# An SSD stage whose VectorE, ScalarE and GpSimd work is ordered by hand, with the decayed state formed one step ahead and one ring of eight PSUM banks

## The chip, the core and the metric

The kernel runs on one NeuronCore of a Trainium2 chip. The metric is the device time of one execution in microseconds. Before the change three runs gave 1432.12, 1432.25 and 1435.49 us, median 1432.25.

## The reference

One layer of a decoder trunk on an input of 1024 rows and 1024 columns, in float32. After a norm with modulation, one wide product makes all branches; a gated spatial mixer and a Mamba-2 state-space part (SSD) follow, and both are projected, gated, summed, projected again and normed. The SSD part works in chunks of 128 rows, for 8 groups of 4 heads (head width 64, state width 128):

```python
xd = (x * dt[..., None]).reshape(b, nc, q, g, r, p)
a_cs = jnp.cumsum(adt, axis=-1)
decay = segsum_exp(adt)
cb = jnp.einsum('bclgn,bcsgn->bcgls', cc, bc)
y_diag = jnp.einsum('bcgls,bcgrls,bcsgrp->bclgrp', cb, decay, xd)
chunk_states = jnp.einsum('bcsgn,bcgrs,bcsgrp->bcgrpn', bc, decay_to_end, xd)
chunk_decay = jnp.exp(a_cs[..., -1])
def step(state, inp):
    cs, cd = inp
    return state * cd[..., None, None] + cs, state
...
y_off = jnp.einsum('bclgn,bcgrpn,bcgrl->bclgrp', cc, prev_states, jnp.exp(a_cs))
```

The output is y_diag + y_off + x * d_skip, multiplied by silu(z) and normed by group. The state of a group runs through its 8 chunks: each new state is the old one times its decay plus the chunk's own sum.

## The kernel before, in words

The program has five stages. Up to about 930 us it norms and modulates the input and forms the wide product; each product is cut into 7 smaller ones (a Strassen scheme, function pair), and every operand is split into a high and a low fp32r half, so that a product is three matmuls. From about 930 to 1150 us runs the **SSD stage**, up to about 1180 us its end, up to about 1335 us the product with w_proj_b (units p1, p2, p5 and so on), and then the output.

The SSD stage is a loop over 32 steps (the list order, L1098). A step is one group and one pair of chunks, i = 0 and 1; two groups alternate, so that a group comes back every second step. A step has these parts:

- fetch (L951, on SP's queue) loads dcy (the cumulated decays, spread over 128 partitions) and sl (B, C, x and z of the step).
- decay (L956): ScalarE forms ea, the exponentials for y_off (L961); GpSimd masks the triangle (affine_select, L964); ScalarE exponentiates dcy in eight pieces (L969).
- prep (L971): TensorE forms the product of B and C and the transposes into the banks pc and px; VectorE multiplies dcy by pc (L989) and x by its two weights, into xd and xe (L985); ScalarE copies bn from pc (L991).
- front (L994): TensorE multiplies yi (the diagonal part, 16 small matmuls) and sp (the two chunk sums). For each of the two new states GpSimd multiplies the old state by its decay (L1017) and VectorE adds sp (L1019). The first state of a group is a copy (L1015).
- back (L1023): TensorE multiplies yn from the states; evacuate (L1036): VectorE forms y1 = x * d_skip + yi (L1045) and ym = yn * ea (L1049); GpSimd adds them (y, L1050) and multiplies by z (yz, L1051).
- post (L1053, every second step of a group): ScalarE's queue stores yz to DRAM (L88); by later(n, ...), a list of due times counted in slots, the squares follow (ScalarE L1069, GpSimd's sum L1070), then a product with ones into pq and the mean ssq (post2, VectorE L1077), and after a group's last pair the power -1/2 on GpSimd (L1081) and a transpose pr of the row (post3).

Between these parts TensorE draws filler (draw): the product of the gated branch with w_proj_a (proj_a; block dd has 48 matmuls into two banks pma, and two loads tha, which VectorE scales by pma at L1270 and ScalarE's queue stores). The weights of the next block are split into wah (ScalarE, L1171) and wal (VectorE, L1172). Behind the loop the last filler (draw(left[0] - 5), and five pieces at the end) runs while the first units of w_proj_b are made ready: load yn and p1r, norm yn (L1376), the halves p1bh, p1bl (L1415, L1416) and p1a (L1420, L1421), then twelve matmuls of a unit into four banks x0 to x3 (L1437).

What sets the order: pin keeps an instruction in program order on its engine. All matmuls and transposes (mm L76, tp L79) and all loads on SP (L85) are pinned. VectorE, ScalarE and GpSimd work of the SSD stage is not pinned: a scheduler orders it at build time by its own estimate of the times, with high_priority for the parts of a step. Whatever the order is, each engine executes its queue strictly in it.

PSUM: the pool ps1 has six banks with the tag bk and two with the tag px. In the SSD stage every fourth call of bank takes a px bank. The states of all groups share four places by turns (st_r). The rings y1_r, ym_r, ea_r, tha_r, war_r, wah_r, wal_r hand out buffers by turns (turn).

Of the kernel before, what the change touches and what calls it, by code (L numbers as in the profile page):

```python
# [8 lines left out]
F32 = mybir.dt.float32  # L9
# [26 lines left out]
def hybrid_kernel(  # L36
# [7 lines left out]
    V, A, G, PE = nc.vector, nc.scalar, nc.gpsimd, nc.tensor  # L44
# [42 lines left out]
    def store(dst, src):  # L87
        nc.scalar.dma_start(dst, src)  # L88
# [478 lines left out]
    pending, pairs_done = [], []  # L567
# [366 lines left out]
    class Group:  # L934


        def __init__(self, g):
            self.g, self.pre, self.st, self.yz, self.y = g, {}, None, {}, {}
# [17 lines left out]
        def decay(self, s):  # L956

            g = self.g
            sl, dcy, ea = self.pre[s]
            for hh in range(2):  # L960
                A.activation(ea[hh * HD : (hh + 1) * HD],  # L961
                             dcy.rearrange("p (j e) i l -> p e j (i l)", e=2)[hh * HD : (hh + 1) * HD, hh], AF.Exp)
            d8 = dcy.rearrange("p h i l -> p (h i) l")
            G.affine_select(out=d8, in_=d8, compare_op=ALU.is_ge, fill=-1e30, base=0,  # L964
                            pattern=[[0, 2 * HPG], [1, P]], channel_multiplier=-1)
            sub = fac(nacs, g, s)
# [4 lines left out]
        def prep(self, s):  # L971
            g, nm = self.g, f"{self.g}_{s}"
# [8 lines left out]
            x4 = px.rearrange("p (i h w) -> p i h w", i=2, h=HPG)  # L981
            xs = []
            for v, f in (("xd", dthq), ("xe", dde)):
                t = p2x.tile([P, 512], F32, name=f"{v}{nm}", tag=v, bufs=3)
                V.tensor_tensor(t.rearrange("p (i h w) -> p i h w", i=2, h=HPG), x4,  # L985
                                fac(f, g, s).unsqueeze(3).to_broadcast([P, 2, HPG, HD]), op=ALU.mult)
                xs.append(t)
            d3 = dcy.rearrange("p h i l -> p h (i l)")
            V.tensor_tensor(d3, d3, pc[:, 0:256].unsqueeze(1).to_broadcast([P, HPG, 256]), op=ALU.mult)  # L989
            bn = p2x.tile([P, 256], F32, name=f"bn{nm}", tag="bn", bufs=3)  # L990
            A.copy(bn, pc[:, 256:512])  # L991
            self.pre[s] = (sl, dcy, bn, xs[0], xs[1], ea)

        def front(self, s):  # L994

            g, nm = self.g, f"{self.g}_{s}"
            sl, dcy, bn, xd, xe, ea = self.pre[s]
            v3 = lambda t: t.rearrange("p (h w) -> p h w", h=HPG)
# [7 lines left out]
            self.y[s] = yi  # L1006
            self.sts = [self.st]
            for i in range(2 if s < NCH // 2 - 1 else 1):
                mm(sp[:, i * 256 : (i + 1) * 256], bn[:, i * P : (i + 1) * P], xe[:, i * 256 : (i + 1) * 256])
            for i in range(2 if s < NCH // 2 - 1 else 1):  # L1010
                pool, tag, b = st_r[nst[0] % 4 if nst[0] % 4 < 3 else 2]
                nst[0] += 1
                s2 = pool.tile([P, 512 if pool is hp else 256], F32, name=f"st{nm}_{i}", tag=tag, bufs=b)[:, 0:256]
                if self.st is None:
                    V.tensor_copy(s2, sp[:, 0:256])  # L1015
                else:
                    G.tensor_mul(v3(s2), v3(self.st),  # L1017
                                 fac(cd, g, s)[:, i].unsqueeze(2).to_broadcast([P, HPG, HD]))
                    V.tensor_add(s2, s2, sp[:, i * 256 : (i + 1) * 256])  # L1019
                self.st = s2  # L1020
                self.sts.append(s2)

        def back(self, s):  # L1023

            sl = self.pre[s][0]
            yn = bank(f"yn{self.g}_{s}")
# [5 lines left out]
            self.evacuate(s, self.y.pop(s), yn)  # L1032
            if s % 2:
                self.post(s // 2)

        def evacuate(self, s, yi, yn):  # L1036

            g, nm = self.g, f"{self.g}_{s}"
            sl, ea = self.pre[s][0], self.pre[s][5]
# [3 lines left out]
            y1 = turn(y1_r, f"y1{nm}", F32).rearrange("p (j t) -> p j t", j=2)  # L1043
            for j in range(2):
                V.scalar_tensor_tensor(y1[:, j], sl[:, 2 + j], dskt[:, 2 * g + j : 2 * g + j + 1],  # L1045
                                       yi[:, j * 256 : (j + 1) * 256], op0=ALU.mult, op1=ALU.add)
# [3 lines left out]
            G.tensor_add(y1[:, :, t0:], y1[:, :, t0:], m[:, :, t0:])  # L1050
            G.tensor_mul(yz, y1, sl[:, 4:6])  # L1051

        def post(self, q):  # L1053

            g = self.g
            for j in range(2):
                store(yb_d[2 * g + j][:, q * 512 : (q + 1) * 512], self.yz[q][:, j])
            yz = self.yz[q]
            if g < NG - 2 or q == 0:
                later(5, self.squares, yz, [yz[:, j] for j in range(2)])  # L1060
                later(17, self.post2, q, yz[:, 0])
            else:
                sq = [turn(r, f"sq{g}", F32) for r in (y1_r, ym_r)]
# [8 lines left out]
        def post2(self, q, sq):  # L1072
            g = self.g
            pq = bank(f"pq{g}_{q}")
            for i in range(4):
                mm(pq[:, i : i + 1], sq[:, i * P : (i + 1) * P], ones[:, 0:1])
            V.tensor_scalar(ssq[:, g * NCH + q * 4 : g * NCH + q * 4 + 4], pq[:, 0:4], 1.0 / 256, EPS,  # L1077
# [7 lines left out]
        def post3(self):  # L1085
# [6 lines left out]
            store(rs_d[g].rearrange("o (c p) -> (o c) p", p=P), row)  # L1092
# [74 lines left out]
    def wa_block(dd):  # L1167
        was[dd] = []
        for i, wr in enumerate(war.pop(dd)):
            wh, wl = turn(wah_r[0], f"wah{dd}_{i}"), turn(wal_r[0], f"wal{dd}_{i}")  # L1170
            A.copy(wh, wr)  # L1171
            V.tensor_sub(wl, wr, f32(wh))  # L1172
            was[dd].append((wh, wl))
# [73 lines left out]
    def proj_a():  # L1247

        for dd in range(KT):
# [8 lines left out]
            for k in range(KT):  # L1258
# [7 lines left out]
                if k == 1 and dd + 1 < KT:  # L1266
                    wa_block(dd + 1)
# [3 lines left out]
            for h in range(2):  # L1271
                keep(nc.scalar.dma_start(mt_d[dd][:, h * 512 : (h + 1) * 512], ths[h]))
# [4 lines left out]
    st_r = [(hp, room.pop(0), 1), (p2x, "st", 1), (p2q, "st", 2)]  # L1277
# [5 lines left out]
    pairs_done.append("")  # L1283
# [22 lines left out]

    draw(6)
# [15 lines left out]


    room.extend(ea_r[0] + [st_r[0][1]])
# [168 lines left out]
    ps1.__exit__(None, None, None)  # L1494
# [18 lines left out]
    for u, (nm, k) in enumerate(units):  # L1513
# [12 lines left out]
        if nm == "p1" and k in (4, 5):  # L1526
            groups[NG - 6 + k].post3()
# [152 lines left out]
```

## Time and profile before

| what | us |
|---|---|
| median of three runs | 1432.25 |
| span of the profiled execution | 1432.7 |
| TensorE busy in it | 1396.2 |
| VectorE, ScalarE, GpSimd busy | 1024.9, 785.1, 205.7 |
| first yi of the SSD stage | 931.90 |
| last yi | 1149.73 |
| first matmul of unit p1 (x) | 1176.17 |
| TensorE idle from 930 to 1150 | 13.5 of 220 |
| TensorE idle from 1150 to 1180 | 4.65 of 30 |

The profiled execution's span is its time from the first to the last instruction; it lies within the range of the three runs. In rows of the timeline the first number is the start and the second the duration, counted from the span's start; in brackets stands the idle time of the engine just before the row and what ended it. In rows of groups the last two parts are busy time with the mean of one, and the idle time before them by releaser. PE is TensorE, DVE is VectorE, ACT is ScalarE, POOL is GpSimd, SP is the queue that issues loads; PEld are weight loads.

### The profile page before, as it was taken

How to read it: one execution, taken by the hardware profiler on the slowest of the kernel's cores; microseconds unless marked ns; L12 is line 12 of the kernel's file. 1: busy time of each engine (PE TensorE's matmuls, PEld its weight loads, DVE VectorE, ACT ScalarE, POOL GpSimd, SP SyncE). 2: the span in 40 equal slices, each digit the busy share in tenths (PEclk: the TensorE clock that was granted, in tenths of full speed). 3: DMA queues.
4: the chain of work that ended last, by engine and by line, in shares of the span. 5: the costliest groups of instructions: out<-in, count | busy, mean ns of one | idle time of the engine just before them, and what ended most of it. 6: DMA issues, size and time to landing. Idle time of an engine off the chain costs nothing.

```text
span 1432.7 us, 20518 instructions
## 1 busy us (share of the span) xinstructions
PE 1396.2 (97%) x7087; PEld 1152.6 (80%) x7087; DVE 1024.9 (72%) x1821; ACT 785.1 (55%) x1444; POOL 205.7 (14%) x190
## 2 busy tenths in 40 slices
PE   8999999999999999999999999999989989999997
PEld 6688888888888888888887888877878877787886
DVE  5686776777667888788887784587677767948443
ACT  6664576566656565555665555776667524325101
POOL 0000000000000000000000100057878830000000
PEclk9999999999999999999999999999999999999999
DMA  8552343333332777687677764788778668977332
GB/s 266 162 162 89 118 118 103 107 100 118 103 114 86 205 223 225 190 246 215 195 231 216 220 180 142 268 297 307 254 262 295 215 211 286 352 254 284 124 118 74
DMA packets 260524, 277.08 MB, mean 193 GB/s; under 512 B 13596, under 2 KB 210628, under 8 KB 260420
## 3 DMA queue, kind: packets, MB, share of 16 engines
q1 hardware_dynamic: 179396, 195.37, 43.8%
q10 hardware_dynamic: 81024, 80.40, 16.6%
q8 instruction: 56, 0.92, 0.3%
q14 instruction: 48, 0.39, 0.1%
HBM read 191.40 MB, written 84.31 MB: 192 GB/s over the span
## 4 chain that ended last, share of the span: by engine, by line
PE 78%; DMA 8%; DVE 5%; issue 3%; ACT 3%; POOL 2%; SPq 1%; ACTq 0%; POOLq 0%; DVEq 0%
PE xuz L563 6%; PE po L76 6%; PE xcb L563 6%; PE xx L563 5%; PE xz L563 5%; PE x L1437 5%; PE xg L563 5%; PE pma L76 3%; PE yp L1437 3%; PE yuz L563 3%; PE xv L563 3%; PE ycb L563 3%; PE yx L563 3%; PE yz L563 2%; PE yg L563 2%
## 5 line engine op out<-in xcount | busy, mean ns | idle before, releaser
L770 POOL TENSOR_TENSOR wog<-wog,gb 128x1024 f32<-128x1024 f32 x8 | 21.8, 2722 | 724.8 <-PE xz L563 529.1
L969 ACT ACTIVATE dcy<-dcy,nacs 128x128 f32<-128x128 f32 x256 | 78.5, 389 | 14.4 <-POOL dcy L964 14.2
L964 POOL TENSOR_SCALAR_AFFINE_SELECT dcy<-dcy 128x1024 f32<-128x1024 f32 x32 | 35.1, 1097 | 107.8 <-ACT ea L961 104.1
L961 ACT ACTIVATE ea<-dcy 64x512 f32<-64x512 f32 x64 | 40.1, 627 | 12.6 <-DMA dcy<-acs_d 12.2
L882 ACT ACTIVATE ac<-ac 128x1024 f32<-128x1024 f32 x32 | 34.0, 1061 | 20.0 <-DVE ac L880 19.8
L1643 ACT ACTIVATE xr<-r 128x1024 f32<-128x1024 f32 x7 | 7.4, 1061 | 67.2 <-issue 39.7
L76 PE MATMUL pma<-yh,wah 128*128 128x512 f32 x128 | 43.9, 424 | 0.0
L76 PE MATMUL pma<-yh,wal 128*128 128x512 f32 x128 | 43.2, 419 | 0.0
L1049 DVE TENSOR_TENSOR ym<-yn,ea 128x512 f32<-128x512 f32 (+1 forms) x32 | 19.9, 623 | 31.3 <-PE yn L76 31.2
L1051 POOL TENSOR_TENSOR yz<-y,sl 128x512 f32<-128x512 f32 x32 | 41.9, 1309 | 1.1
L989 DVE TENSOR_TENSOR dcy<-dcy,pc 128x1024 f32<-128x1024 f32 x32 | 39.0, 1217 | 4.3 <-PE pc L79 3.0
L76 PE MATMUL pma<-yl,wah 128*128 128x512 f32 x128 | 40.5, 398 | 0.0
L76 PEld LDWEIGHTS yn<-sl,st 128*128 128x128 f32 x224 | 30.3, 190 | 10.9 <-POOL yz L1051 2.9
L1050 POOL TENSOR_TENSOR y<-y,ym 128x512 f32<-128x512 f32 (+1 forms) x32 | 36.5, 1142 | 16.3 <-DVE ym L1049 16.3
L1633 POOL TENSOR_TENSOR r<-r,fnw 128x256 f32<-128x256 f32 (+1 forms) x3 | 2.7, 916 | 250.7 <-ACT xr L1632 250.7
L76 PE MATMUL yn<-sl,st 128*128 128x128 f32 x224 | 31.7, 276 | 7.1 <-DVE st L1019 7.1
L880 DVE SCALAR_TENSOR_TENSOR ac<-c2x,cwt,ac 128x1023 f32<-128x1023 f32 (+2 forms) x24 | 31.8, 1325 | 9.0 <-ACT ac L878 7.1
L1642 DVE TENSOR_TENSOR r<-po,xr 128x1024 f32<-128x1024 f32 x7 | 8.6, 1225 | 41.1 <-PE po L76 41.1
L76 PE MATMUL sp<-xe,bn 128*128 128x256 f32 x112 | 33.0, 411 | 4.5 <-DVE ym L1049 1.4
L76 PE MATMUL yi<-dcy,xd 128*64 128x128 f32 x512 | 35.9, 284 | 0.0
L880 DVE SCALAR_TENSOR_TENSOR ac<-c2cb,cwt,ac 128x1023 f32<-128x1023 f32 (+2 forms) x24 | 30.6, 1275 | 7.1 <-ACT ac L878 7.0
L1017 POOL TENSOR_TENSOR st<-st,cd 128x256 f32<-128x256 f32 x48 | 32.3, 673 | 10.3 <-PE yn L76 7.2
(2827 smaller groups left out, 4395.4 us busy)
## 6 DMA issues: line engine op xcount, KB each, us to landing
sl<-s_d SPq DMA_DIRECT2D x32, 768.0 KB
s_d<-ac ACTq DMA_DIRECT2D x32, 512.0 KB
dcy<-acs_d SPq DMA_DIRECT2D x32, 512.0 KB
aw<-in_ada_w_dram SPq DMA_DIRECT2D x16, 512.0 KB
wbr<-in_w_proj_b_dram SPq DMA_DIRECT2D x64, 128.0 KB
wb_d<-wbb ACTq DMA_DIRECT2D x32, 256.0 KB
wb_d<-wbc ACTq DMA_DIRECT2D x32, 256.0 KB
yb_d<-yz ACTq DMA_DIRECT2D x32, 256.0 KB
```

The costliest lines, as they stand in the source:

```text
L76: pin(PE.matmul(acc, l, r, start=first, stop=last))
L563: pin(PE.matmul(ps, lw[:, k * P : (k + 1) * P], r[k], start=first and n + k == 0, stop=n == 2 and k == 3, skip_group_check=not first))
L880: V.scalar_tensor_tensor(ac[:, s:], cc[:, : S - s], conv_wt[:, 3 - s, i : i + 1], ac[:, s:], op0=ALU.mult, op1=ALU.add)
L882: A.activation(ac, ac, AF.Silu)
L961: A.activation(ea[hh * HD : (hh + 1) * HD], dcy.rearrange("p (j e) i l -> p e j (i l)", e=2)[hh * HD : (hh + 1) * HD, hh], AF.Exp)
L964: G.affine_select(out=d8, in_=d8, compare_op=ALU.is_ge, fill=-1e30, base=0, pattern=[[0, 2 * HPG], [1, P]], channel_multiplier=-1)
L969: A.activation(dcy[:, h, i, :], dcy[:, h, i, :], AF.Exp, bias=sub[:, i, h : h + 1])
L989: V.tensor_tensor(d3, d3, pc[:, 0:256].unsqueeze(1).to_broadcast([P, HPG, 256]), op=ALU.mult)
L1017: G.tensor_mul(v3(s2), v3(self.st), fac(cd, g, s)[:, i].unsqueeze(2).to_broadcast([P, HPG, HD]))
L1050: G.tensor_add(y1[:, :, t0:], y1[:, :, t0:], m[:, :, t0:])
L1051: G.tensor_mul(yz, y1, sl[:, 4:6])
L1437: pin(PE.matmul(ps[j], a[:, v, js], r, start=first and n + k == 0, stop=n == 2 and k == KT - 1, skip_group_check=not first))
```

## The change

- A wrapper Engine passes every instruction that VectorE, ScalarE and GpSimd issue inside the SSD loop through pin, as long as hand[0] is true: their order is then that of the program text (in the changed kernel's profile such an instruction has the line of the wrapper).
- decay is split into decay_rows (ea and the mask) and decay_exps, prep into prep_products (with dcy and xd), prep_b (bn) and prep_xe. The loop issues them at set places: decay_rows of step n+3 first, then front of n, xe of n+1, back of n, prep_products of n+2, decay_exps of n+3, prep_b of n+2.
- y1 is formed in front, straight behind yi, no longer in evacuate.
- The decayed state is formed one step ahead: front adds sp to a state that GpSimd has decayed before (self.nxt), and GpSimd at once decays it for chunk 1; back adds chunk 1's sum behind ym, and GpSimd decays the result for the group's next step, ahead of yz. There are five places for states instead of four.
- At the start of the stage ps1 is closed and a pool ps2 with one ring of eight banks is opened; it is laid on the same banks.
- Stores of yz, mt_d and rs_d are issued through later, squares after 9 slots instead of 5, the mean ssq one slot behind its product, and wal two filler pieces behind wah.

The core of the diff:

```diff
-    V, A, G, PE = nc.vector, nc.scalar, nc.gpsimd, nc.tensor
+    hand = [False]
+    class Engine:
+        def __getattr__(self, name):
+            f = getattr(self.e, name)
+            if not hand[0]:
+                return f
+            return lambda *a, **k: tc.keep_in_program_order(f(*a, **k))
+    V, A, G, PE = Engine(nc.vector), Engine(nc.scalar), Engine(nc.gpsimd), nc.tensor
...
-        if pairs_done:
-            pairs_done.append(name)
-            if len(pairs_done) % 4 == 2:
-                return psum.tile([P, 512], F32, name=name, tag="px", bufs=2)
-        return psum.tile([P, 512], F32, name=name, tag="bk", bufs=6)
+        return psum.tile([P, 512], F32, name=name, tag="bk", bufs=n_banks[0])
...
+    def decayed(self, dst, s, i):
+        v3 = lambda t: t.rearrange("p (h w) -> p h w", h=HPG)
+        G.tensor_mul(v3(dst), v3(self.st), fac(cd, self.g, s)[:, i].unsqueeze(2).to_broadcast([P, HPG, HD]))
...
+            if self.st is None:
+                self.st = self.state(f"st{nm}_0")
+                V.tensor_copy(self.st, sp[:, 0:256])
+            else:
+                self.st = self.nxt
+                V.tensor_add(self.st, self.st, sp[:, 0:256])
+            self.sts.append(self.st)
+            self.nxt = None
+            if not last:
+                self.nxt = self.state(f"st{nm}_1"), sp
+                self.decayed(self.nxt[0], s, 1)
...
+            if self.nxt is not None:
+                self.st, sp = self.nxt
+                V.tensor_add(self.st, self.st, sp[:, 256:512])
+                self.nxt = self.state(f"st{nm}_2")
+                self.decayed(self.nxt, s + 1, 0)
             G.tensor_mul(yz, y1, sl[:, 4:6])
...
-    pairs_done.append("")
+    ps1.__exit__(None, None, None)
+    ps2 = tc.tile_pool(name="ps2", bufs=1, space=PSUM, reuse_waits="tile")
+    psum = ps2.__enter__()
+    n_banks[0] = 8
...
+    hand[0] = True
     draw(6)
     for n in range(2):
         step(n, "front")
         draw(10)
-    for n in range(len(order)):
+    for n in range(N):
+        ahead3 = 0 < n < N - 3
+        if ahead3:
+            of(n + 3, "decay_rows")
         if n > 1:
             step(n, "front")
             draw(10 if n == 2 else 4 + n % 2)
+        if 0 < n < N - 1:
+            of(n + 1, "prep_xe")
         step(n, "back")
-        if n + 2 < len(order):
-            step(n + 2, "prep")
+        if n + 2 < N:
+            step(n + 2, "prep_products")
+        if ahead3:
+            of(n + 3, "decay_exps")
+        if n + 2 < N:
+            of(n + 2, "prep_b")
         fetch(n + 6)
-        decays(n + 4)
     while tasks:
         draw(2)
         run_tasks()
+    hand[0] = False
```

More of the change, by code (lines that the diff above doesn't have):

```diff
@@ L965, in decay, with decay_exps @@
                             pattern=[[0, 2 * HPG], [1, P]], channel_multiplier=-1)
-            sub = fac(nacs, g, s)
+        def decay_exps(self, s):
+            dcy = self.pre[s][1]
+            sub = fac(nacs, self.g, s)
             for i in range(2):
@@ L1042, in evacuate @@
             yz = self.yz[s // 2][:, :, (s % 2) * 256 : (s % 2 + 1) * 256]
[L1043 to L1046, printed above, removed]
+            y1 = self.y.pop(s)
             m = turn(ym_r, f"ym{nm}", F32).rearrange("p (j t) -> p j t", j=2)
@@ L1305, in step, with of @@
             item(getattr(groups[order[n][0]], f), order[n][1])
+    N = len(order)
+    def of(n, f):
+        g, s = order[n]
+        getattr(groups[g], f)(s)
+    hand[0] = True
     draw(6)
@@ L1526, in hybrid_kernel @@
         if nm == "p1" and k in (4, 5):
-            groups[NG - 6 + k].post3()
+            groups[NG - 6 + k].post3(True)
         if k % 2 and nm in GATES:
```

132 lines of the change are left out of this document (81 added, 51 removed).

## Prediction

> **What bounds the kernel now.** I read the page first, then the table of stretches, then TensorE's waits in the SSD stage, and last the timeline around each wait.
>
> ```profile
> span 1432.7 us, 20518 instructions
> PE 1396.2 (97%) x7087; PEld 1152.6 (80%) x7087; DVE 1024.9 (72%) x1821; ACT 785.1 (55%) x1444; POOL 205.7 (14%) x190
> ```
>
> The span lies 0.45 us above the median of the three runs (1432.25). I work against the span and take 0.45 off at the end. TensorE is busy 97%, so only its idle time can be won. The stretches (busy us of PE, PEld, DVE, ACT, POOL, then the granted clock) tell where that is:
>
> ```profile
> 930.00:1150.00 220.00, 206.48 (x1548) 178.87 (x1548) 163.32 (x294) 145.70 (x378) 162.45 (x158) 0.99 0.78 268
> 1150.00:1180.00 30.00, 25.35 (x136) 21.09 (x133) 17.04 (x32) 9.30 (x17) 11.96 (x8) 0.94 0.70 229
> 1180.00:1335.00 155.00, 153.86 (x656) 122.66 (x655) 115.31 (x185) 57.63 (x98) 0.00 (x0) 1.00 0.83 287
> ```
>
> The change touches the first two rows: 13.5 us idle in 220, and 4.65 in the 30 where the stage runs out. The product stage behind it is full, so it can neither hide a delay nor give time back. TensorE's waits from 925 to 1180 (releaser: total, times, longest):
>
> ```profile
> PE yn L76 <- DVE st L1019: 7.1, 6, 2.7
> PE pq L76 <- POOL sq L1070: 4.6, 1, 4.6
> PE pc L76 <- issue: 1.9, 1, 1.9
> PE sp L76 <- DVE ym L1049: 1.4, 1, 1.4
> PE sp L76 <- DVE xe L985: 1.2, 2, 0.6
> PE sp L76 <- DVE ssq L1077: 1.0, 1, 1.0
> PE sp L76 <- DVE st L1019: 0.9, 1, 0.9
> ```
>
> All but pq sum to 13.5: half are products that wait for a new state, the rest mostly PSUM banks that VectorE has not yet read. The timeline (start, duration) gives the frame and a second cost:
>
> ```profile
> 931.90 1.09 PE L76 MATMUL yi<-dcy,xd 128*64 128x128 f32 x16
> 949.18 0.46 PE L76 MATMUL pc<-sl 128*128 128x128 f32 x2 [1.90 <-issue]
> 984.53 0.68 PE L76 MATMUL yn<-sl,st 128*128 128x128 f32 x4 [2.72 <-DVE st L1019]
> 986.61 1.98 PE L76 MATMUL yi<-dcy,xd 128*64 128x128 f32 x16
> 1041.99 0.68 PE L76 MATMUL yn<-sl,st 128*128 128x128 f32 x4 [2.34 <-DVE st L1019]
> 1149.73 1.09 PE L76 MATMUL yi<-dcy,xd 128*64 128x128 f32 x16
> ```
>
> After the 2.72 us wait the same sixteen yi products take 1.98 instead of 1.09: the granted clock fell. With the matmuls beside them I put the loss at 1.6 us, an estimate. After 2.34 us nothing was lost. First to last yi is 217.8 us for 31 steps; without 13.5 and 1.6 it is 202.7, **6.54 us a step**, the floor that TensorE's own work sets.
>
> **The change part by part.** Instructions per engine are the same in kind and number; only order, banks and waits differ.
>
> (1) *The state one step ahead.* GpSimd multiplies the old state by its decay before the sum it belongs to exists, so yn waits only for one addition. In the built program yi(n) now waits for xe(n), sp(n) for ym(n-1), each read a step earlier. What does a step cost the other engines? The groups from 950 to 1150 (29 steps; total, mean ns):
>
> ```profile
> L1051 POOL TENSOR_TENSOR yz<-y,sl 128x512 f32<-128x512 f32 x29 | 38.0, 1311 | 1.0
> L1017 POOL TENSOR_TENSOR st<-st,cd 128x256 f32<-128x256 f32 x44 | 29.9, 679 | 8.2 <-PE yn L76 6.5 <-DVE st L1015 1.1 <-DVE st L1019 0.6
> L964 POOL TENSOR_SCALAR_AFFINE_SELECT dcy<-dcy 128x1024 f32<-128x1024 f32 x27 | 29.6, 1097 | 19.3 <-ACT ea L961 19.3
> L1050 POOL TENSOR_TENSOR y<-y,ym 128x512 f32<-128x512 f32 x22 | 28.1, 1278 | 12.7 <-DVE ym L1049 12.7
> L1050 POOL TENSOR_TENSOR y<-y,ym 128x256 f32<-128x256 f32 x7 | 5.1, 734 | 0.2 <-DVE ym L1049 0.2
> L1070 POOL TENSOR_TENSOR yz<-yz 128x512 f32<-128x512 f32 x14 | 18.0, 1283 | 4.0 <-ACT yz L1069 3.4 <-DVE st L1019 0.5
> L1081 POOL TENSOR_TENSOR ssq<-ssq,nhalf 128x8 f32<-128x8 f32 x6 | 9.9, 1653 | 0.0
> L1049 DVE TENSOR_TENSOR ym<-yn,ea 128x512 f32<-128x512 f32 x23 | 15.9, 690 | 28.0 <-PE yn L76 28.0
> L1019 DVE TENSOR_TENSOR st<-st,sp 128x256 f32<-128x256 f32 x45 | 18.5, 413 | 10.3 <-POOL st L1017 9.8 <-PE sp L76 0.4
> L989 DVE TENSOR_TENSOR dcy<-dcy,pc 128x1024 f32<-128x1024 f32 x29 | 35.3, 1217 | 3.8 <-PE pc L79 2.5 <-issue 0.7 <-ACT yz L1069 0.2
> L1045 DVE SCALAR_TENSOR_TENSOR y<-sl,dskt,yi 128x256 f32<-128x256 f32 x58 | 25.0, 473 | 0.0
> L1270 DVE SCALAR_TENSOR_TENSOR tha<-tha,pma 128x512 f32<-128x512 f32 x12 | 7.8, 682 | 0.9 <-PE pma L76 0.9
> ```
>
> And from the timeline, xd and xe of step 1, one behind the other:
>
> ```profile
> 935.27 0.68 DVE L985 TENSOR_TENSOR xd<-px,dthq 128x512 f32<-128x512 f32 x1
> 935.87 0.67 DVE L985 TENSOR_TENSOR xe<-px,dde 128x512 f32<-128x512 f32 x1
> ```
>
> GpSimd's rows sum to 158.6 us over 29, or 5.47 a step. VectorE's loop from one yn to the next, in the new order, is ym 0.69, state 0.41, dcy 1.22, xd 0.68, two y1 0.95, state 0.41: 4.36, against 6.54 less yn's own 0.9, or 5.65. Both fit, so the 13.5 and the 1.6 go: **-15.1**.
>
> (2) *What the fixed order leaves.* In seven steps the two tha (1.36) stand in that loop: 4.36 + 1.36 is 5.72, over by 0.07, and by up to 0.7 with xe behind them. In three steps squares (1.28) and the power (1.65) meet on GpSimd: the affine 1.10, two decays 1.36, y 1.28, yz 1.31 and these are 7.98, 1.44 over 6.54; the state addition st1 on VectorE then waits, with dcy, xd and the next yn behind it. Bounds: 0 to 7 x 0.7 + 3 x 1.44 = 9.2. I take half of what the sp rows above show for standing behind other reads in VectorE's queue (1.4 + 1.2 + 1.0): **+1.8**, nearer to the lower bound because the lead of one step absorbs single late operations.
>
> (3) *The start.* The new ring is laid over banks that are still in use. In the built program the second pma bank waits for step 0's copy bn, and yi of step 0 waits for xe of step 1, which before it did not.
>
> ```profile
> 931.08 0.35 ACT L991 COPY bn<-pc 128x256 f32<-128x256 f32 x1
> ```
>
> So one pma matmul runs early, as before, and the other eleven start at 931.45 (idle some 2.1) and end at 934.0; that xe ends at 936.54 (its row is above), so yi comes at 936.6 (idle 2.6) instead of 931.90: **+4.7**. VectorE's order up to that xe is unchanged. The 1.90 at 949.18 lies behind it and is swallowed; I leave +0.3 of it. The 2.6 lies between 2.34 (no loss of clock) and 2.72 (1.6 lost): half, **+0.8**. Bounds +3 (xe moves up) to +6.6. The Trainium skill ("TensorE: Matmul & The Clock Gate", the section on what is actually happening) states that the gate closes after an idle window of about 3.4 us; by that no wait here costs clock and the sum is 0.8 lower. This trace does not agree: 2.72 us was enough.
>
> (4) *The end of the stage.* ACT's last squares now stand ahead of its p1 casts, and GpSimd's sum of squares ahead of the power, so pq no longer waits 4.65. What is late next is x. The rows:
>
> ```profile
> 1156.41 0.32 SPq L85 DMA_DIRECT2D yn<-yb_d  x1
> 1166.06 0.32 SPq L85 DMA_DIRECT2D yn<-yb_d  x1
> 1169.44 1.28 PE L76 MATMUL pq<-ones,sq 128*128 128x1 f32 x8 [4.65 <-POOL sq L1070]
> 1170.83 0.75 DVE L1376 SCALAR_TENSOR_TENSOR yn<-yn,par,rb 128x512 f32<-128x512 f32 x1
> 1176.17 0.39 PE L1437 MATMUL x<-p1bh,p1a 128*128 128x512 f32 x1
> ```
>
> In the new VectorE order the norm of unit 4 (the row at 1170.83) and a small ssq stand before p1a of unit 0, which x0 needs: 1170.83 + 0.67 + 0.15 + 0.68 = 1172.3. Ten more operations, 0.60 apart like xd and xe above (935.27, 935.87), stand before the second tha of block 7, whose bank x3 takes over: 1178.3. Nine matmuls of 0.23 come before x3, so unit 0 ends as if it had begun at 1176.2, no earlier than before. And TensorE has then idled some 4 us, which by the slow matmuls behind the 4.65 wait (eighteen pma took 5.6 instead of 4.1) costs 1.5 more: **+1.7**. Bounds: -6.2 (4.65 and 1.5 both gone) to +4.1: SP issues unit 0's load only behind the last yn, so one unit more, 2.4 apart by SP's issues of the units 1 to 5, whose first and last are the rows at 1156.41 and 1166.06, stands ahead of unit 4's.
>
> (5) *At nothing:* stores moved past exponentials on ACT's queue (ACT is busy 145.7 of 220), the low halves of w_proj_a two filler steps later, five state places instead of four, the bank ring itself. SP issues in the same order. VectorE's and ACT's spare time covers them; without it each costs at most its own 0.3 to 0.7 us a few times, inside the range of (2).
>
> Sum: 1432.7 - 15.1 + 1.8 + (4.7 + 0.3 + 0.8 = 5.8) + 1.7 = 1426.9; less 0.45 is **1426.5**.
>
> **Rivals.** (A) *Nothing is lost at the end:* unit 4's data are there early (its row shows no idle time before it, which speaks for this) and the scheduler's order does not bind. No clock loss, no residue in (2) but 0.5: 1432.7 - 15.1 + 5.0 + 0.5 - 6.2 = 1416.9, less 0.45: 1416.5; mixtures lie up to 1422. Against it: ten operations stand before x3 whatever the loads do.
>
> (B) *GpSimd becomes the bound,* slower. Pinned, it must also sit out its waits: y for ym (12.7 over 22, 0.58) and the early decay for st1 (0.41): 5.47 + 0.99 = 6.46, just under 6.54. Its operations can stretch beside others:
>
> ```profile
> 950.29 1.61 POOL L1051 TENSOR_TENSOR yz<-y,sl 128x512 f32<-128x512 f32 x1
> 1168.19 1.75 DVE L1421 TENSOR_TENSOR p1a<-p1r,p1a 128x512 fp32r<-128x512 f32 x1
> ```
>
> The first is 1.61 against a mean of 1.31. If the fixed order stretches GpSimd's operations by 10% on average, the step is 7.0 and 31 x 0.46 = 14.3 takes the place of (2): 1439.4, less 0.45: 1439. It decides from 6.54 us on. For it: the load. Against: the mean 1311 holds such cases already, and GpSimd has waits that other work can fill. The Trainium skill ("GPSIMD Engine Reference", Specifications) states that GpSimd shares its SBUF interfaces with VectorE and suffers beside VectorE operations with two SBUF inputs; of the loop's only the wal halves are such, and the stretched p1a above agrees. By that rule the pinned order adds little and (B) is less likely.
>
> (C) *The early state buys little,* the change not doing what it says: the waits move from yn to reads behind tha and the power, (2) at its upper end of 9.2: 1432.7 - 15.1 + 9.2 + 5.8 + 1.7 = 1434.3, less 0.45: 1434. For it: before's sp rows; against: one step of lead.
>
> **How the numbers follow.** 0.3% (4.3 us: 1428.0 to 1436.5) is about what a measurement of this kernel can tell from no change. Forecast 0.48, with a range of its own of 1422.5 to 1430.5, so 0.34 faster and 0.14 same; A 0.22 (faster); C 0.14 (same); B 0.16 (slower). Faster 0.56, same 0.28, slower 0.16. A range of 1416 to 1437 leaves out most of B and a little of A.
>
> **What the new profile would show.** (1) right: yn waits for st near zero, yi starts 6.5 us apart; wrong if they stay over 6.8. (2): single sub-microsecond waits in steps with tha or a power. (3): two waits of 2 to 3 us at pma and yi before 937, and yi of step 3 some 3 us later than 959. (4): no wait of pq on sq, instead x waiting for p1a and tha for about 4 us in all. The prediction is wrong if GpSimd is busy nearly throughout the stage, or if x follows pma without a wait.

## The result, and the profile after

| kernel | runs | median us (lowest to highest) | ratio to before [95% interval] |
|---|---|---|---|
| before | 4 | 1433.71 (1432.12 to 1435.49) | |
| after | 4 | 1427.98 (1427.42 to 1432.24) | 0.9967 [0.9953, 0.9982] |

The change makes the kernel 0.33% faster, some 4.7 us by the ratio. The ratio and its interval are estimated from all runs of the group and are not the quotient of the two medians, which lie 5.7 us apart. The prediction said 1426.5 with a range of its own of 1422.5 to 1430.5; the median of after lies inside. The profiled execution of after is the slowest of its four: span 1430.5, where the other three have 1425.7 to 1426.7. Two more profiles of the same code are among the experiments (e0, e7), so that what is peculiar to the profiled execution can be told from what the change does.

The page of after, its span and busy times:

```profile
span 1430.5 us, 20475 instructions
PE 1400.6 (98%) x7087; PEld 1154.9 (81%) x7087; DVE 1027.8 (72%) x1821; ACT 782.0 (55%) x1444; POOL 204.9 (14%) x190
```

The stretches of after, columns as in the prediction (busy us of PE, PEld, DVE, ACT, POOL, then granted clock, DMA share, GB/s):

```profile
930.00:1150.00 220.00, 213.64 (x1583) 184.30 (x1584) 166.78 (x297) 144.56 (x379) 164.82 (x160) 0.98 0.77 267
1150.00:1180.00 30.00, 25.84 (x124) 21.06 (x123) 19.64 (x35) 10.09 (x19) 8.76 (x6) 0.94 0.76 259
1180.00:1335.00 155.00, 152.63 (x644) 121.38 (x643) 113.17 (x182) 55.62 (x96) 0.00 (x0) 0.99 0.80 282
```

TensorE's idle time from 930 to 1150 is halved (6.4 us of 220 instead of 13.5). TensorE's waits of after from 925 to 1185 (releaser: total, times, longest) show which went:

```profile
PE x L1525 <- DVE tha L1335: 3.5, 1, 3.5
PE pma L90 <- ACT bn L1019: 1.8, 1, 1.8
PE yn L90 <- POOL st_home L56: 1.4, 2, 0.9
PE yi L90 <- DVE xe L1013: 1.4, 1, 1.4
PE yn L90 <- DVE st_home L56: 1.3, 2, 0.9
PE pq L90 <- POOL sq L56: 0.6, 1, 0.6
```

The 7.1 us of yn behind a state are down to 2.7 (two rows, both named st_home), and pq waits 0.6 instead of 4.6. New are x behind tha, and pma and yi at the start. The timeline of after at the start:

```profile
928.76 0.49 PE L90 MATMUL pma<-yh,wah 128*128 128x512 f32 x1
931.02 0.50 PE L90 MATMUL pma<-yh,wah 128*128 128x512 f32 x1 [1.76 <-ACT bn L1019]
...
932.30 0.97 PE L90 MATMUL pma<-yh,wah 128*128 128x512 f32 x2
...
936.34 1.98 PE L90 MATMUL yi<-dcy,xd 128*64 128x128 f32 x16 [1.36 <-DVE xe L1013]
...
942.66 0.63 PE L90 MATMUL pma<-yh,wah 128*128 128x512 f32 x2
```

These are the two waits of step (3), at their places: one pma matmul goes early, the next waits for bn, and yi waits for xe of step 1. But TensorE slows down already at 932.30 (0.97 for a pair that takes 0.63 at 942.66) and stays slow for 10 us; the granted clock from 932 to 943 is 0.53.

At the end of the stage, TensorE's timeline of after, then VectorE's:

```profile
1160.82 1.05 PE L90 MATMUL pq<-ones,sq 128*128 128x1 f32 x8 [0.64 <-POOL sq L56]
1165.91 0.39 PE L1525 MATMUL x<-p1bh,p1a 128*128 128x512 f32 x1
...
1171.70 0.79 PE L1525 MATMUL x<-p1bh,p1a 128*128 128x512 f32 x1 [3.52 <-DVE tha L1335]
```

```profile
1164.15 0.75 DVE L1464 SCALAR_TENSOR_TENSOR yn<-yn,par,rb 128x512 f32<-128x512 f32 x1
1164.81 0.15 DVE L56 TENSOR_SCALAR ssq<-pq 128x4 f32<-128x4 f32 x1
1164.88 0.68 DVE L1509 TENSOR_TENSOR p1a<-p1r,p1a 128x512 fp32r<-128x512 f32 x1
...
1170.97 0.67 DVE L1335 SCALAR_TENSOR_TENSOR tha<-tha,pma 128x512 f32<-128x512 f32 x1
```

This is the order that the prediction named: the norm of unit 4, the small ssq, p1a of unit 0, and then the operations up to the second tha, 6.09 us after p1a (ten of 0.60 were forecast). x0 goes 10.3 us earlier than before and follows the last filler without a wait; x3 stops for 3.52 us behind that tha, and its first matmul takes 0.79 instead of 0.39.

In the product stage, where nothing was changed, TensorE and VectorE of after:

```profile
1217.29 0.47 PE L1525 MATMUL yp<-p5bh,p5a 128*128 128x512 f32 x1 [0.89 <-ACT p5bh L1503]
...
1219.10 0.79 PE L1525 MATMUL yp<-p5bh,p5a 128*128 128x512 f32 x1 [0.89 <-DVE c L1635]
```

```profile
1214.63 0.75 DVE L1464 SCALAR_TENSOR_TENSOR yn<-yn,par,rb 128x512 f32<-128x512 f32 x1 [0.41 <-DMA yn<-yb_d]
...
1216.50 0.69 DVE L1635 TENSOR_TENSOR c<-c,yp 128x512 f32<-128x512 f32 x1
```

p5 overwrites the banks of p2, which VectorE reads with four additions c; the first stands behind the norms of p5's later units, and one of these waits for its load. Before, p5 began without a wait (22.49 us behind the first matmul of p2) and met the additions once, for 0.63 us; the rows of before stand in the section on the prediction.

Where the time went, stretch by stretch. The marks are rows of TensorE's timeline: the first matmul of xg<-t4h,p4g14h (the last product ahead of the stage), the first and the last yi, and the first matmuls of p1, p2, p5 and p3. Before has them at 925.08, 931.90, 1149.73, 1176.17, 1198.88, 1221.37 and 1244.74, and ends at 1432.7. The table gives each stretch of before, and for the other profiles the difference to it; the experiments follow below.

| profile | to xg | xg to yi | yi to last yi | to p1 | p1 to p2 | p2 to p5 | p5 to p3 | rest | span |
|---|---|---|---|---|---|---|---|---|---|
| before | 925.08 | 6.82 | 217.83 | 26.44 | 22.71 | 22.49 | 23.37 | 187.96 | 1432.7 |
| after | -0.45 | +4.89 | -9.61 | -5.09 | +5.13 | +1.05 | +1.87 | +0.01 | -2.2 |
| e0 (after) | +1.25 | +4.38 | -12.59 | -5.00 | +7.16 | +0.07 | +0.34 | -0.01 | -4.4 |
| e7 (after) | +1.30 | +4.88 | -11.05 | -5.07 | +6.30 | 0 | +0.31 | -0.07 | -3.4 |
| e1 | +0.40 | +4.92 | +49.41 | -0.32 | +6.18 | +2.59 | +2.81 | +0.11 | +66.1 |
| e2 | +1.08 | +4.27 | +0.65 | -0.75 | +0.70 | 0 | 0 | +0.55 | +6.5 |
| e3 | -0.96 | +4.90 | -2.01 | +0.97 | 0 | 0 | -0.16 | -0.04 | +2.7 |
| e4 | -1.69 | 0 | -9.83 | -5.04 | +6.02 | +0.73 | +0.33 | +0.38 | -9.1 |
| e10 (as e4) | +0.07 | 0 | -9.87 | -4.97 | +5.37 | +1.31 | +1.81 | -0.02 | -6.3 |
| e5 | -0.61 | +4.26 | -12.53 | -5.04 | +1.25 | +6.19 | +1.19 | +0.59 | -4.7 |
| e6 | +1.03 | 0 | -9.85 | -5.04 | +0.92 | +5.65 | +1.84 | -0.05 | -5.5 |
| e9 | +1.05 | 0 | -9.65 | -4.97 | +5.20 | +1.69 | +1.88 | +0.50 | -4.3 |
| e8 | -0.17 | 0 | -9.86 | -4.97 | +0.38 | +5.33 | +1.60 | +0.69 | -7.0 |
| e11 | +0.10 | 0 | -9.44 | -5.08 | -0.01 | +2.38 | +1.03 | +9.62 | -1.4 |

The first column, which no edit touches, moves by 3 us from execution to execution. So single spans say little within 2 or 3 us; the stretches say more, and the medians decide between kernels. The profile of before is itself at the low end: in the groups of runs below the medians of before lie between 1433.78 and 1436.33.

### The profile page after: what moved, and what is told of

It is laid out like the page before. It is cut to its first block, busy times and chain, and to the rows that moved or that the text cites. A ratio compares the mean times of both kernels' runs of the same rounds, so it can differ in the third digit from the quotient of the medians.

```text
span 1430.5 us, 20475 instructions
## 1 busy us (share of the span) xinstructions
PE 1400.6 (98%) x7087; PEld 1154.9 (81%) x7087; DVE 1027.8 (72%) x1821; ACT 782.0 (55%) x1444; POOL 204.9 (14%) x190
## 4 chain that ended last, share of the span: by engine, by line
PE 73%; DMA 8%; DVE 6%; ACT 5%; issue 4%; POOL 3%; SPq 1%; ACTq 0%; POOLq 0%; DVEq 0%
PE xuz L573 6%; PE po L90 6%; PE xcb L573 6%; PE xx L573 5%; PE xz L573 5%; PE x L1525 4%; PE yp L1525 3%; PE yuz L573 3%; PE pma L90 3%; PE xv L573 3%; PE ycb L573 3%; PE yx L573 3%; PE xg L573 2%; PE yz L573 2%; DMA yn<-yb_d 2%
## 5 line engine op out<-in xcount | busy, mean ns | idle before, releaser
L56 ACT ACTIVATE dcy<-dcy,nacs 128x128 f32<-128x128 f32 x224 | 68.6, 388 | 31.8 <-POOL dcy L56 15.6
L1464 DVE SCALAR_TENSOR_TENSOR yn<-yn,par,rb 128x512 f32<-128x512 f32 x32 | 24.5, 765 | 16.0 <-DMA yn<-yb_d 15.9
L56 ACT ACTIVATE ea<-dcy 64x512 f32<-64x512 f32 x56 | 35.2, 629 | 1.3 <-DMA dcy<-acs_d 1.0
L56 POOL TENSOR_SCALAR_AFFINE_SELECT dcy<-dcy 128x1024 f32<-128x1024 f32 x28 | 32.0, 1141 | 18.3 <-ACT ea L56 17.6
L90 PEld LDWEIGHTS yi<-dcy,xd 128*64 128x64 f32 x512 | 28.1, 139 | 6.9 <-issue 4.7
L56 DVE SCALAR_TENSOR_TENSOR y<-sl,dskt,yi 128x256 f32<-128x256 f32 x64 | 27.7, 473 | 7.7 <-PE yi L90 4.3
```

The lines of the kernel that those rows point to most:

```text
L56: return lambda *a, **k: tc.keep_in_program_order(f(*a, **k))
L90: pin(PE.matmul(acc, l, r, start=first, stop=last))
L1464: V.scalar_tensor_tensor(t, t, snw[:, n : n + 1], rbs[n // 2, h], op0=ALU.mult, op1=ALU.mult)
```

## The experiments

The time of a run is the median of its group of runs. All ratios are against before in the same group, estimated as in the table of the result.

**e0 and e7: the changed kernel again,** no edit.

> The changed kernel once more, unedited, as the yardstick for the runs beside it. If the 4.5 us between its profiled run (span 1430.5) and its other runs (spans 1425.7 to 1426.7) are clock lost behind the two waits of the first step and behind a wait at the first p5 unit, a profiled run of about 1426 shows full clock from 932 to 943 and from 1217 to 1223; one of about 1430 shows it lowered there. If the difference lies elsewhere, those stretches look alike in both.

> The changed kernel unedited, as the yardstick for the three bank edits of this call: 1426 to 1429 us, or up to 1432 where the clock falls at the start.

e0: 1428.99 us, ratio 0.9958 [0.9935, 0.998]. e7: 1429.51 us, 0.9964 [0.995, 0.9978]. The wait of pma for bn is there each time. The wait of yi for xe is 1.36 in after, absent in e0 and 2.5 in e7, and the loss of clock varies with it: yi takes 1.98, 1.09 and 1.80 us. The timeline of e0 at this place:

```profile
933.26 0.50 PE L90 MATMUL pma<-yh,wah 128*128 128x512 f32 x1 [1.75 <-ACT bn L1019]
...
934.84 1.05 PE L90 MATMUL pma<-yh,wah 128*128 128x512 f32 x2
...
937.53 1.09 PE L90 MATMUL yi<-dcy,xd 128*64 128x128 f32 x16
```

Here the slow pma matmuls fill the time in which xe gets ready, and the clock is back with yi. The granted clock from 932 to 943 is 0.53 in after and 0.84 in e0 and e7; around p5 it is 0.72 in after (1217 to 1223) and 1.00 in e0 (1213 to 1223). So e0's profile, between the two cases of its expectation in time, has the clock lowered at the first place and full at the second. The start costs 4.3 to 4.9 us in every profile whose ring begins as in after (after, e0, e7, e1, e2, e3, e5), and the clock up to 3 more, not alike from execution to execution: the stretch from first to last yi is 205.24, 206.78 and 208.22 us for the same code.

**e1: the state decayed at its own step.** Order by hand and ring stay; GpSimd's product of state and decay is issued straight ahead of the addition it belongs to.

```diff
-                self.st = self.nxt
+                dst = self.state(f"st{nm}_0")
+                self.decayed(dst, s, 0)
+                self.st = dst
                 V.tensor_add(self.st, self.st, sp[:, 0:256])
...
-                self.st, sp = self.nxt
-                V.tensor_add(self.st, self.st, sp[:, 256:512])
-                self.nxt = self.state(f"st{nm}_2")
-                self.decayed(self.nxt, s + 1, 0)
+                dst = self.state(f"st{nm}_1")
+                self.decayed(dst, s, 1)
+                self.st = dst
+                V.tensor_add(self.st, self.st, self.nxt[:, 256:512])
```

> Hand order and ring of eight stay; the decayed state is formed directly ahead of its addition again, where it stood before the change. Theory (forming it one step ahead removes the waits of yn): yn waits for the state again in most steps, the decay standing on GpSimd behind yz and the squares, 8 to 30 us above the changed kernel. Rival (the order and the ring do it, the early state nothing): within 2 us of the changed kernel.

1500.86 us, ratio 1.0457 [1.042, 1.0495]: slower than before, and by more than any theory had it. TensorE's waits of e1:

```profile
PE yn L90 <- DVE st L56: 22.7, 11, 4.0
PE yn L90 <- DVE st_home L56: 18.4, 8, 4.0
```

One of them on GpSimd, VectorE and TensorE of e1, in this order:

```profile
1000.05 1.09 POOL L56 TENSOR_SCALAR_AFFINE_SELECT dcy<-dcy 128x1024 f32<-128x1024 f32 x1 [1.97 <-ACT ea L56]
1001.11 0.61 POOL L56 TENSOR_TENSOR st<-st,cd 128x256 f32<-128x256 f32 x1
```

```profile
1001.75 0.42 DVE L56 TENSOR_TENSOR st<-st,sp 128x256 f32<-128x256 f32 x1 [1.97 <-POOL st L56]
```

```profile
1002.23 1.01 PE L90 MATMUL yn<-sl,st 128*128 128x128 f32 x3 [3.91 <-DVE st L56]
```

In this fixed order the decay stands behind the mask of a later step, and the mask waits for ScalarE's ea. VectorE waits for the decay and TensorE for VectorE. Twelve of the fourteen waits of yn over 1 us have these rows in front of them, with 1.97 to 2.44 us of waiting at the mask. With 19 waits of 2.2 us on average the clock falls as well: 0.91 on average from 925 to 1205. With the loop issued as it is, the early state is what makes the fixed order bearable. A fixed order written for the late decay (with the decay ahead of the mask, say) was not run.

**e2: early state and ring, order left to the scheduler.**

```diff
-    hand[0] = True
     draw(6)
```

> Early state and ring of eight stay; the scheduler orders VectorE, ScalarE and GpSimd again. Theory (the early state carries most of the gain, the fixed order little): within 4 us of the changed kernel, few waits of yn. Rival (the order set by hand is what removes the waits): 8 us or more above the changed kernel, near the kernel before, with waits of sp and yn behind reads that stand late in VectorE's queue.

1440.05 us, ratio 1.0037 [1.0019, 1.0055]. My theory, that the early state alone brings most of the gain, falls: the stage is as long as before (+0.65). TensorE's waits of e2:

```profile
PE pq L90 <- POOL sq L1118: 3.9, 1, 3.9
PE yn L90 <- DVE st L1062: 3.7, 2, 3.1
PE yn L90 <- POOL st_home L1035: 2.2, 1, 2.2
```

The scheduler puts some of the decays late again, and pq waits as before; so the wait at pq went by the fixed order, as step (4) had it.

**e3: only the ring of eight banks, in the kernel before.**

```diff
-        if pairs_done:
-            pairs_done.append(name)
-            if len(pairs_done) % 4 == 2:
-                return psum.tile([P, 512], F32, name=name, tag="px", bufs=2)
-        return psum.tile([P, 512], F32, name=name, tag="bk", bufs=6)
+        return psum.tile([P, 512], F32, name=name, tag="bk", bufs=n_banks[0])
...
-    pairs_done.append("")
+    ps1.__exit__(None, None, None)
+    ps2 = tc.tile_pool(name="ps2", bufs=1, space=PSUM, reuse_waits="tile")
+    psum = ps2.__enter__()
+    n_banks[0] = 8
```

> The kernel before with one edit, the ring of eight. Theory (laying the ring over banks in use costs the first step some 5 us and more with the clock; in the steps a ring of eight removes at most the waits of sp and pc, 5.5 us): between 2 us faster and 6 us slower than the kernel before, the two waits of the first step in place and the waits of yn for the state still about 7 us. Rival (the banks were the main limit): 8 us or more faster.

1438.36 us, ratio 1.0016 [0.9998, 1.0035]: as expected a little slower or the same. The start costs +4.90, as in after; the stage gains 2.0 (the bank waits are gone, yn still waits for st, 10.8 us in all). So neither the ring alone, nor the ring with the fixed order (e1), nor the ring with the early state (e2) is a gain; the gain came only with fixed order and early state together. Not run: these two without the ring, and the smaller parts taken back alone, that is the moved stores, the later squares and the low halves wal (which come six draws of filler behind wah, three for each k, and not two).

**e4 and e10: the ring begins four places later.** Four small copies take the first four banks, so that the first step gets banks that are free by then.

```diff
     n_banks[0] = 8
+    for k in range(4):
+        V.tensor_copy(bank(f"skip{k}")[:, 0:1], ones[:, 0:1])
```

> The changed kernel with four small copies of one column into the first four tiles of the new ring, ahead of the loop, so that pma, yi and sp of the first step get banks that are free (the products that follow are the same). Theory (the overlay costs 4.9 us at the first step, 2.9 more where the clock falls): the waits of pma on bn and of yi on xe are gone, first yi near 931.5, and 4 to 8 us less than the changed kernel at the last yi; the end of the stage is as before or a little better, since now x2 waits for the first tha of block 7. Rival (time won ahead of the w_proj_b product is given back to its loads): less than 2 us in all.

> The start's bank edit unedited once more, as the yardstick for the two runs beside it: 1424.6 to 1429.9 us.

e4: 1426.19 us, ratio 0.9943 [0.9927, 0.9958]. e10: 1427.60 us, 0.9959 [0.9945, 0.9973]. Both waits at the start and the loss of clock there are gone (granted clock 1.00 up to 943), and yi comes 6.82 us behind xg, as before the change. Half of this is lost some 15 us later, and these rows of e10's TensorE and that of its VectorE say to what:

```profile
948.12 0.44 PE L93 MATMUL px<-ident,sl 128*128 128x128 f32 x2 [1.99 <-DVE tha L56]
...
949.13 1.06 PE L90 MATMUL yn<-sl,st 128*128 128x128 f32 x4
```

```profile
947.38 1.39 DVE L56 SCALAR_TENSOR_TENSOR tha<-tha,pma 128x512 f32<-128x512 f32 x2 [1.73 <-DMA tha<-th_d]
```

px takes over a bank that tha has to read, and tha now waits for its load (in e0 it waits for pma there). Behind this wait e10 loses clock too: four yn matmuls take 1.06 us at 949.13, and 0.60 at 945.20. e4 has nearly the same wait (1.93) and loses no clock. From first to last yi e4 and e10 need 208.0 us, where e0 needs 205.2. Of the 4 to 8 us expected at the last yi, 1.6 to 5.1 came in e4 against the three profiles of after (first column left out). What is left is small: beside e7, in the same group of runs, the median of e4 is 3.3 us lower; that of e10, in another group, lies 0.4 to 1.9 us under the three of after; all the intervals overlap with one of after's. Of the kernels with the four copies e4, e6, e8, e9 and e10 lie 0.4 to 0.6% under before and e11 0.2%; after, e0 and e7 lie 0.3 to 0.4% under it.

**e5, e6: the banks of the first product.** In e5 x and yp take the banks by turns, so that x3 no longer takes over the second tha's bank; e6 has this in another order ("xxxyxyyy") together with the four copies of e4.

```diff
-                psy = banks("yp2", "y")
-                psx = banks("x", "x")
+                psx, psy = [], []
+                for c in "xyxyxyxy":
+                    p = psx if c == "x" else psy
+                    j = len(p)
+                    p.append(psb.tile([P, 512], F32, name=f"{c if c == 'x' else 'yp2'}{j}", tag=f"b{c}{j}"))
```

> The changed kernel with the banks of the x and yp tiles interleaved, so that no x tile takes over a bank of pma of block 7; order on all engines unchanged. Theory (x3 waits 3.5 us for tha only because of the bank, and 1.5 us of clock behind it): the wait of x on tha goes and 3 to 5 us are won at unit 1 of p1; of these up to 2 come back as waits for p1 and p5 operands. Rival (loads and VectorE's splits bind p1 right behind it): the wait only moves to units 1 to 4 of p1, less than 1.5 us in all.

> Both bank edits together. Theory (two separate losses): the sum of the two gains, 6 to 12 us less than the changed kernel, about 1417 to 1421 us, unless the w_proj_b product's loads bind. Rival (loads bind): no faster than the better of the two alone.

e5: 1430.01 us, ratio 0.9969 [0.9957, 0.9981]. e6: 1428.98 us, 0.9956 [0.9941, 0.9972]. The wait of x is gone (p1 to p2 +1.25 and +0.92 instead of +5 to +7), and p5 hands all of it back (p2 to p5 +6.19 and +5.65) where the theory of e5 had up to 2 us coming back. e6 is no faster than e4, as its rival had it. The rows of e5, VectorE and then TensorE:

```profile
1212.24 0.75 DVE L1464 SCALAR_TENSOR_TENSOR yn<-yn,par,rb 128x512 f32<-128x512 f32 x1 [0.41 <-DMA yn<-yb_d]
...
1214.11 0.68 DVE L1638 TENSOR_TENSOR c<-c,yp 128x512 f32<-128x512 f32 x1
```

```profile
1214.89 0.76 PE L1525 MATMUL yp<-p5bh,p5a 128*128 128x512 f32 x1 [5.39 <-issue]
```

The profile names no releaser for this wait (issue), but p5 starts 0.1 us behind the end of the first c. c keeps its place in VectorE's queue, behind norms that wait for loads, whenever TensorE arrives. Two causes were open: the loads come too late, or only VectorE's order is in the way.

**e8, e9: the loads earlier.** SP's queue stood still in e5 from 1177.74 to 1187.33, because the load rb behind it needs the rows rs_d of the last groups, made at units 4 and 5 of p1. e8 is e6 and e9 is e4 with these rows at units 2 and 3.

```diff
-        if nm == "p1" and k in (4, 5):
-            groups[NG - 6 + k].post3(True)
+        if nm == "p1" and k in (2, 3):
+            with tc.high_priority():
+                groups[NG - 4 + k].post3(True)
```

> Both bank edits, and the transposes of the last two groups' norm rows (post3, which SP's load of rb waits for with all later loads behind it) behind unit 2 and 3 of p1 instead of 4 and 5. Theory (what the bank edits won at x came back as the wait of p5, because SP's queue stood from 1176 to 1187 behind that load): the gap in SP's queue shortens by 4 us or more, the wait at the first p5 unit falls from 5 us to under 3, and the time is 2 to 5 us below both bank edits alone, about 1424. Rival (the bytes of these loads bind, whenever they are issued): the gap shortens and the time stays within 1 us.

> The start's bank edit and the earlier rows, with the x banks as in the changed kernel. Theory: the wait of x2 for tha stays at 3 us, the loads of p2 and p5 come earlier; 0 to 3 us below the start's bank edit alone (about 1423 to 1426). Rival (bytes bind): within 1 us of it.

e8: 1427.29 us, ratio 0.9954 [0.9938, 0.9969]. e9: 1426.60 us, 0.9952 [0.9938, 0.9966]. Beside e10 in the same group (1427.60) both are the same. SP's queue in e5 and in e8, around its gap:

```profile
1176.36 1.38 SPq L99 DMA_DIRECT2D p2r<-in_w_proj_b_dram  x1
1187.33 0.32 SPq L99 DMA_DIRECT2D rb<-rs_d  x1
```

```profile
1174.40 1.75 SPq L99 DMA_DIRECT2D p2r<-in_w_proj_b_dram  x1
1182.35 0.32 SPq L99 DMA_DIRECT2D rb<-rs_d  x1
```

The queue issues nothing for 9.6 us in e5, 9.3 in e6 and 6.2 in e8, 3.1 less than in e6 where 4 or more were expected, and p5's wait shrinks only from 4.9 us (e6) to 3.7 (e8), not to under 3. The time came out as the rivals had it (e8 by its ratio beside e6's, e9 by 1.0 us under e10, which its theory allowed as well); e11 shows that its reason, the bytes, is not the one that holds p5.

**e11: the additions first.** On top of e8 the four additions c are pinned ahead of p5's unit 3, and VectorE's and ScalarE's operands from p5 on keep program order.

```diff
         multiply(u, ps)
+        if nm == "p2" and k == KT - 1:
+            for j in range(4):
+                pin(V.tensor_add(more[j][2], more[j][2], psy[j]))
         ahead(u)
...
-        keep = pin if u < 4 else lambda i: i
+        keep = pin if u < 4 or u >= 2 * KT else lambda i: i
...
```

> Against e8_both_rows, p5 still begins 4 us after the last product of p2, in a wait of 3.7 us and one of 0.9 us: its banks are read by VectorE's four additions c (L1641, from 1211.30), which stand behind the norms of p5's units 4 to 7, and two of these wait for their loads (1.04 and 0.49 us). Here the four additions stand straight behind unit 2 of p5, and VectorE's operands of p5 and p3 keep the order of the program text; as a side effect the halves of p3's units 6 and 7 come ahead of those of 3 to 5. Theory (order of VectorE's queue): the four additions begin within 0.7 us of the end of p2, the wait at p5 falls from 3.7 us to under 1.3 and p2 to p5 from 27.8 us to under 25.5; p5 to p3 stays under 25.0 us. Rival (the loads bind, wherever VectorE stands): p2 to p5 falls, but units 3 to 7 of p5 then wait for their loads, so that p2 to p3, 52.8 us in e8, stays over 51.5. In both cases p3 to p6 may be over 22.5 us by up to 4 through the side effect, so the time says little: 1424 to 1431.

1432.57 us, above the 1424 to 1431 expected; ratio 0.998 [0.9964, 0.9995]. VectorE of e11 where p2 ends, and its stretches:

```profile
1207.41 2.79 DVE L1622 TENSOR_TENSOR c<-c,yp 128x512 f32<-128x512 f32 x4 [0.57 <-PE yp L1529]
```

```profile
1200.00:1220.00 20.00, 20.00 (x87) 16.10 (x86) 13.12 (x20) 2.71 (x5) 0.00 (x0) 1.00 1.04 398
1220.00:1240.00 20.00, 18.93 (x77) 13.58 (x75) 18.58 (x30) 7.57 (x14) 0.00 (x0) 1.00 0.96 357
1240.00:1260.00 20.00, 13.59 (x49) 9.81 (x48) 19.16 (x32) 4.33 (x7) 0.00 (x0) 0.91 0.35 107
```

p5 begins without a wait now, TensorE is full from 1200 to 1220 beside a DMA share of 1.04, and p2 to p3 takes 49.27 us (52.79 in e8), under the 51.5 that the rival set: the order of VectorE's queue held p5, not the bytes. (Of the +2.38 in p2 to p5, 2.0 us are a wait of p2 for its own p2bl.) The side effect is larger than I had put it: VectorE comes to p3 with its work out of order, is busy 19.16 of 20 us, and p3bl waits cost TensorE 6.7 us and clock; the rest is +9.62. A version with the additions early and p3 in order was not run.

## Why the prediction was right, and where it was off

The forecast was right in its main step and in the time; a part of the closeness is luck, since terms that were off cancel. In spans it forecast -5.8 us against before; the three profiles of the changed kernel give -2.2, -4.4 and -3.4, and without the first column, which the change doesn't touch, -1.75, -5.65 and -4.7.

1. **The steady part** (-15.1 + 1.8, and +0.3 + 0.8 of step (3): together -12.2). Measured from first to last yi: -9.61, -12.59, -11.05. The steps are 6.62 to 6.72 us long, between the 6.5 forecast and the 6.8 that would have spoken against it. Most of the waits of yn for a state went. What is left in the profile of after up to the last yi is 2.4 of yn and 1.3 of yi and px, 3.7 us where 1.8 + 0.3 were put; they stand, as forecast, in single waits under 1 us. The clock at the start was mis-sized: 0.8 was put, and 2.9 (yi and the matmuls behind it, up to 942.66), about nothing and some 1.6 us came out in after, e0 and e7. With idle time and this loss taken off, TensorE's own work in the stretch is 201.6 us in all three, 1.1 less than the floor of 202.7. Where the 1.1 comes from is open; it hides most of the 1.6 that the remaining waits are over their term.
2. **The start** (+4.7): +4.89, +4.38 and +4.88. Of the two waits named, 2.1 and 2.6 in the forecast, e7 has 1.76 and 2.49, after 1.76 and 1.36, and e0 only the first, 1.75: in these two slow pma matmuls, which the forecast did not have ahead of yi, fill the time up to xe. e4 and e10 take the cause away, and the 4.9 us with it.
3. **The end of the stage** (+1.7, columns "to p1" and "p1 to p2" together): +0.04, +2.16 and +1.23. In the profile of after unit 4's norm came at 1164.15, where 1170.83 was put, mostly because the whole stage ended earlier (the last yi by 5.2 us); the distance from p1a to the second tha (6.09 us) was right. The clock behind the wait, put at 1.5 us, came to 1.6 in after, 3.0 in e0 and 2.1 in e7 (p1 to p2 less the wait at x3 of 3.52, 4.17 and 4.17). One sign did not come as written: x0 did not wait for p1a and followed pma without a wait, which the prediction had named as a sign of being wrong; the whole wait came at x3, for tha.
4. **"The product stage can neither hide a delay nor give time back":** this step is wrong. A busy time of 153.86 in 155 us says that TensorE was hardly kept waiting when it came late, not that VectorE and the loads had slack. When TensorE comes 4 to 15 us earlier, p5 meets additions that stand behind norms: +2.9 us in the profile of after, +0.3 to +0.4 in e0 and e7, and some 7 us (the two columns from p2 to p3) as soon as the wait at x goes (e5, e6, e8). For the change itself it cost little, since the wait of x3 stood ahead of it. Before has the same crowding, with TensorE arriving late enough to meet 0.63 us of it. In VectorE of before the first c again stands behind a norm (from 1218.87); it and the wait of TensorE are these rows:

```profile
1220.26 0.68 DVE L1547 TENSOR_TENSOR c<-c,yp 128x512 f32<-128x512 f32 x1
```

```profile
1222.86 0.51 PE L1437 MATMUL yp<-p5bh,p5a 128*128 128x512 f32 x1 [0.63 <-DVE c L1547]
```

The stretch 1200 to 1220 of before and of after:

```profile
1200.00:1220.00 20.00, 20.00 (x87) 16.05 (x87) 15.86 (x25) 7.12 (x13) 0.00 (x0) 1.00 1.03 384
```

```profile
1200.00:1220.00 20.00, 18.23 (x76) 14.12 (x75) 17.93 (x29) 5.84 (x10) 0.00 (x0) 0.98 1.03 396
```

The rivals. (A), nothing lost at the end, did not come: x3 waits 3.5 to 4.2 us in all three profiles. (B), GpSimd as the bound, did not come: of its three large groups from 950 to 1150, below, only the mask is longer, by 4%. The groups of GpSimd in after (total, mean ns):

```profile
L56 POOL TENSOR_TENSOR yz<-y,sl 128x512 f32<-128x512 f32 x31 | 39.8, 1284 | 0.5
L56 POOL TENSOR_SCALAR_AFFINE_SELECT dcy<-dcy 128x1024 f32<-128x1024 f32 x28 | 32.0, 1141 | 18.3 <-ACT ea L56 17.6 <-PE sp L90 0.6
L56 POOL TENSOR_TENSOR y<-y,ym 128x512 f32<-128x512 f32 x23 | 29.4, 1277 | 11.1 <-DVE ym L56 11.1
```

Before they were 1311, 1097 and 1278. (C), little bought by the early state, is what e2 shows for the early state without the fixed order; in the fixed order the waits do not move on to the reads. What the prediction did not see is how much its first term hangs on both parts: it credited the early state with the gain, while the early state without the fixed order is 11 us slower than e0 (e2), and the fixed order of this loop without the early state 72 (e1).

## What to carry to other kernels

Here a fixed order and early production belonged together: in a queue of fixed order, whatever an operation of the loop needs must be ready before its place comes, or every engine behind it waits (e1). A new pool laid over banks in use charges the first step (4.3 to 4.9 us here); begin its ring at the banks that come free first, and look at which bank is taken over next, since half of the gain was lost there. Before counting on time won ahead of a stage that looks full, ask what the other engines of that stage would do if it began earlier; here the next queue was a few us behind.

## What the runs showed of the hardware

The granted clock fell after short idle times, and not always. The same wait of pma at the start, 1.76 us in after, 1.75 in e0 and 1.76 in e7, was followed by slow matmuls within 1.3 us in after and e0, and by none in e7 until a second wait of 2.49 us. TensorE stayed slow for 10 us in after, where a wait of 1.36 fell into that time, and for under 4 in e0. The same wait of px was followed by slow matmuls in e10 (1.99 us) and by none in e4 (1.93). In before, 2.72 us (984.53) cost clock and 2.34 us (1041.99) did not. Two waits of 0.89 us with three matmuls between them were followed by slow matmuls in after (1217.29 to 1219.10). The Trainium skill ("TensorE: Matmul & The Clock Gate", What's actually happening) says that the gate watches a free-running window of some 3.4 us, so that the same code meets it at different points. That the same wait cost clock in one execution and not in another agrees with that; that an idle time as long as the window is needed does not agree with these rows.
